# Layer 0 of a two-layer decoder trunk: transposes by VectorE's 32x32 blocks and a DRAM scratch in place of TensorE

## The chip, the cores and the metric

The kernel runs on one core of one Trainium2 chip, in one launch. The metric is the device time of that core in microseconds: the median of the runs, beside one profiled execution, whose times the trace holds. The engines named below are TensorE (PE; its weight loads are shown apart as PEld), VectorE (DVE), ScalarE (ACT), GpSimd (POOL) and SyncE (SP), which issues nearly all DMAs.

## The reference, cut to what matters

Two decoder layers over 256 tokens of width 2048, in float32. Each layer is a token mixer and a gated MLP with a width-3 causal convolution on its gate branch (width 5632), each behind an RMS norm and with a residual. Layer 0's mixer, the one that is changed, is causal attention with 16 heads of 128 (the block-sparse form of the reference falls together with it, since 256 tokens are one block):

```python
q = rope(rms_norm((h @ wq).reshape(B, S, H, dh), gq), pos, rot)   # rot = 32
k = rope(rms_norm((h @ wk).reshape(B, S, H, dh), gk), pos, rot)
v = (h @ wv).reshape(B, S, H, dh)
...
p = jax.nn.softmax(s, axis=-1)       # s = q k^T * dh**-0.5, causal
o = p @ v                            # and then o @ wo
```

Layer 1's mixer is latent attention (low-rank queries, keys and values with a shared rotary key). It has transposes of its own and is not changed.

## The kernel before, in words

TensorE multiplies float32 here in three products: a weight is split into a high part (ScalarE's copy to fp32r, L125) and a rest (VectorE's subtraction, L126), activations likewise, and hi x hi, hi x lo and lo x hi are summed. The weights come as 370 units of up to 1 MB, each of four pieces of 128x512. `Stream` (L70) loads units through SP into three buffers (L90) and splits pieces into five pairs of buffers.

The order is written out by hand. A quantum is what TensorE does with one piece: in layer 0's projections `tok_major` (L254), two token tiles by three products, six matmuls; in the output projection and the MLP `feat_major` (L278), twelve matmuls of 256 columns. The loop at the end of `trunk` (L1199) goes through the quanta: it first splits pieces up to four ahead, then issues the quantum's matmuls, then whatever has been planned for this quantum: `at(q, f)` puts f behind quantum q, `first_in(q, rank, f)` puts it there too, but ahead of the others. Every engine takes its instructions in this order. So a planned step that is not ready holds up what is planned behind it on its own engine, the splits of later pieces included.

Layer 0 goes in four groups of four heads; each has 16 quanta for queries, 16 for keys, 16 for values. Behind the last quantum q of queries or keys stands `plan_heads` (L677): `evac` takes the sums out of PSUM into a tile x of 128 tokens x 2 tiles x 4 heads x 128 (q), squares (q+1, q+2) and `rstd` (q+3, GpSimd's power) make the head norms, `scaled` and `rotate` follow at q+6 to q+9. At q+11 `turned` (L480) has TensorE transpose the eight 128x128 blocks of x into PSUM, and `queries_out` or `keys_out` (L643, L652) copy from there: a high part and a rest, and one plain copy for the first 128 tokens. For the first group everything stands some quanta later.

For each head `Head.plan` (L593) places at q the scores (TensorE) and `biased` (mask and row minimum, VectorE), at q+1 the exponentials (ScalarE), at q+2 `normal` (VectorE), at q+6 `turn` (three TensorE transposes of the probabilities, L566) with `turned` (L569: copies and the rest), and at q_values `values` (products with the values) and `parted` (the output split in two parts for the next projection). In the first three groups two heads share a place, the second pair six quanta after the first, and the values stand 12 quanta after the scores. In the last group the heads come two quanta apart and run into the output projection, the values at least 8 quanta after the scores. The output projection takes heads 0 to 7 of its first eight tiles before heads 8 to 11 and then 12 to 15.

PSUM holds four accumulators, two banks for scores and values (`sc`) and two for transposes (`tp`).

Of the kernel before, what the change touches and what calls it, by code (L numbers as in the profile page):

```python
# [10 lines left out]
F32 = mybir.dt.float32  # L11
# [3 lines left out]
ALU = mybir.AluOpType  # L15
PSUM = bass.MemoryType.PSUM

P = 128
S = 256
D = 2048  # L20
NT = S // P
# [115 lines left out]
def trunk(ctx: ExitStack, tc: tile.TileContext, a, out):  # L137
    nc = tc.nc
# [5 lines left out]
    ps_acc = ctx.enter_context(tc.tile_pool(name="ps_acc", bufs=4, space=PSUM))  # L144
    ps_tp = ctx.enter_context(tc.tile_pool(name="ps_tp", bufs=2, space=PSUM))
    ps_sc = ctx.enter_context(tc.tile_pool(name="ps_sc", bufs=2, space=PSUM))
    ctx.enter_context(tc.manual_schedule())

    mm = nc.tensor.matmul
# [90 lines left out]
    def at(q, f, *args):  # L240
        side.setdefault(q, []).append((f, args))
# [4 lines left out]
    def first_in(q, rank, f, *args):  # L246
        leading.setdefault(q, [[], []])[rank].append((f, args))
# [133 lines left out]
        nc.sync.dma_start(out[:, j, :], xT[:, j, :])  # L381


    class Heads:


# [65 lines left out]
        def rotate(self, t, stages=range(4)):  # L452
            if not self.rot:
                return
            n, rot = self.n, self.rot
            hf = rot // 2
            tb, C, Sn = self.tabs
            ct = tb[:, C + t * rot : C + (t + 1) * rot]
            st = tb[:, Sn + t * rot : Sn + (t + 1) * rot]
            x = self.x[:, t]  # L460
            def over(s):
                return s[:, None, :].to_broadcast([P, n, s.shape[1]])

            def part(name):
                r = att_pool.tile([P, 16 * 32], F32, name=name, bufs=2)
                return r[:, : n * rot].rearrange("p (n r) -> p n r", n=n)

            if 0 in stages:
                self.rot_parts = part("ro1"), part("ro2")
            t1, t2 = self.rot_parts  # L470
            if 0 in stages:
                nc.vector.tensor_tensor(t1, x[:, :, :rot], over(ct), op=ALU.mult)
            if 1 in stages:
                nc.vector.tensor_tensor(t2[:, :, :hf], x[:, :, hf:rot], over(st[:, :hf]), op=ALU.mult)
            if 2 in stages:
                nc.vector.tensor_tensor(t2[:, :, hf:], x[:, :, :hf], over(st[:, hf:]), op=ALU.mult)
            if 3 in stages:
                nc.vector.tensor_tensor(x[:, :, :rot], t1, t2, op=ALU.add)

        def turned(self, dst, pair, i0):  # L480

            tp = ps_tp.tile([P, 512], F32, name="tp")
            flat = self.x.rearrange("p t n d -> p t (n d)")
            for i in range(2):
                for t in range(NT):
                    c = (i0 + i) * P
                    nc.tensor.transpose(  # L487
                        tp[:, (i * NT + t) * P : (i * NT + t + 1) * P], flat[:, t, c : c + P], ident
                    )
            pair["tp"] = tp  # L490
# [8 lines left out]
    class Head:  # L499
# [32 lines left out]
                mm(second, qr[:, P:], kr[:, part], start=False, stop=part == 1, **flags)  # L532

        def biased(self):
            self.s = att_pool.tile([P, 3 * P], F32, name="s", bufs=3)
            self.st = small.tile([P, 6], F32, name="sst")
            masked = mask
            if self.apart:
                masked = self.s
                nc.vector.tensor_tensor(self.s[:, :P], self.sc[:, 3 * P :], mask[:, :P], op=ALU.add)  # L540
            for c, n, k, m in ((P, S, 1, mask), (0, P, 0, masked)):
                nc.vector.tensor_tensor_reduce(
                    out=self.s[:, c : c + n], in0=self.sc[:, c : c + n], in1=m[:, c : c + n],
                    scale=1.0, scalar=3e38, op0=ALU.add, op1=ALU.min,
                    accum_out=self.st[:, k : k + 1],
                )
# [16 lines left out]
        def turn(self):  # L563
# [2 lines left out]
                nc.tensor.transpose(tp[:, c * P : (c + 1) * P], self.s[:, c * P : (c + 1) * P], ident)  # L566
            self.tp = tp

        def turned(self):  # L569

            self.pT = att_pool.tile([P, 2, S], F32R, name="pT", bufs=2)
            self.pT1 = att_pool.tile([P, P], F32, name="pT1", bufs=2)
            hi, lo = self.pT[:, 0], self.pT[:, 1]
            nc.scalar.copy(hi, self.tp[:, :S])
            nc.scalar.copy(self.pT1, self.tp[:, S : 3 * P])
            nc.vector.tensor_tensor(lo, self.tp[:, :S], hi.bitcast(F32), op=ALU.subtract)

        def values(self):
            o = ps_sc.tile([P, 512], F32, name="sc")
# [13 lines left out]
        def plan(self, q, q_values, q_turn=None):  # L593


            q_turn = q_turn or q + 6
            at(q, self.scores)
            at(q, self.biased)

            late = self.rope is not None  # L600
            at(q + 1 + (late and q_turn == q + 6), self.exps)
            at(q + 2 + late + (late and q_turn == q + 6), self.normal)
            first_in(q_turn, 1, self.turn)
            first_in(q_turn, 1, self.turned)
            first_in(q_values, 0, self.values)
            first_in(q_values, 0, self.parted)
# [5 lines left out]
    env = {}  # L612
# [39 lines left out]
    def keys_out(dst, tp, i0, gain=None):  # L652
# [5 lines left out]
        copied(k0[i0 // 2], src[:, :, :P], gain)  # L658
        rest_of(lo, src, hi, gain)

    def evac_parts(state, key, scale):
        v0, v1 = env[key]
        hi, lo = v0[:, 0], v0[:, 1]
        first_, second = (state["acc"][t][:, :512] for t in range(NT))
        if scale is None:
            nc.scalar.copy(hi, first_)
            nc.vector.tensor_tensor(lo, first_, hi.bitcast(F32), op=ALU.subtract)
            nc.scalar.copy(v1, second)
            return
        r = scale()  # L670
        nc.scalar.activation(hi, first_, AF.Copy, scale=r[:, 0:1])
        nc.vector.scalar_tensor_tensor(
            lo, first_, r[:, 0:1], hi.bitcast(F32), op0=ALU.mult, op1=ALU.subtract
        )
        nc.scalar.activation(v1, second, AF.Copy, scale=r[:, 1:2])

    def plan_heads(q, hs, key, out):  # L677

        at(q, hs.evac)
        for t in range(NT):  # L680
            at(q + 1 + t, hs.squares, t)
        at(q + 3, hs.rstd)
        for t in range(NT):
            at(q + 6 + 2 * t, hs.scaled, t)
            at(q + 7 + 2 * t, hs.rotate, t)
        for i0 in (0, 2):
            pair = {}
            q1 = q + 11
            at(q1, lambda hs=hs, p=pair, i0=i0: hs.turned(None, p, i0))
            at(q1, lambda p=pair, i0=i0, key=key: out(env[key], p["tp"], i0))  # L690

    at(-1, n1.scaled, 0)
    def signed_gains():
# [11 lines left out]
    for g in range(4):  # L705
        for kind in "qkv":
            state = {"first": g == 0 and kind == "q"}
            for kt in range(KD):
                q = add(tok_major, state, lambda: n1.h, kt, KD - 1)
                if g == 0 and kind == "q" and kt + 1 < KD:  # L710
                    first(q + 1, n1.scaled, kt + 1)
                if g == 0 and kind == "k" and kt < 12:
                    for j in range(kt * 4 // 3, (kt + 1) * 4 // 3):
                        at(q, n1.square, j)
                        at(q + 1, n1.total, j)
            if g == 0 and kind == "q":
                at(q + 14, n1.sums)
            if kind == "q":
                at(q, moba_tiles, g)
            if kind == "v":  # L720
                at(q, evac_parts, state, ("v", g), lambda: n1.rstd)
                q_v = q
            else:
                hs = Heads(state, 4, P, G_Q if kind == "q" else G_K, 32, (tab, T_MC, T_MS), lambda: n1.rstd)
                plan_heads(q + (0 if g else 15 if kind == "q" else 9), hs, ("qT" if kind == "q" else "kT", g),
                           queries_out if kind == "q" else keys_out)
                q_k = q
        for i in range(4):
            hd = Head(
                4 * g + i, lambda g=g: env["qT", g], lambda g=g: env["kT", g], lambda g=g: env["v", g],  # L730
                i, lambda: env["oT"], parts=True,
            )
            if g < 3:

                q0 = q_k + (14 if g else 22) + i // 2 * 6
                hd.plan(q0, q0 + 12)
            else:
                q0 = q_k + 14 + 2 * i
                hd.plan(q0, max(q0 + 8, q_v + 3 + i))


    def plan_wo(norm, order):
# [301 lines left out]
    class Rotary:  # L1044
# [6 lines left out]
        def out(self, i):  # L1051
            heads = env["qrT"][:, 4 * (self.i0 // 2) + 2 * i : 4 * (self.i0 // 2) + 2 * i + 2]
            tp = self.pair["tp"].rearrange("p (a s) -> p a s", a=2)
            rows, rest = (slice(k * 64, (k + 1) * 64) for k in (i, 1 - i))
            nc.scalar.copy(heads[rows], tp[rows])
            nc.vector.tensor_tensor(heads[rest], tp[rows], heads[rows].bitcast(F32), op=ALU.subtract)
# [263 lines left out]
```

## Time and profile before

| What | Value |
|---|---|
| median of three runs | 2083.99 us (2083.98 to 2084.32) |
| profiled execution, its span | 2081.8 us |
| TensorE busy | 2076.9 us, 16742 matmuls |
| VectorE busy | 1415.0 us (68%) |
| ScalarE busy | 1148.0 us (55%) |
| DMA | 391.82 MB, of it 2.10 MB written to HBM |
| granted TensorE clock | 1.000 |

The span runs from the first to the last instruction. Layer 0's projections and heads lie at about 0 to 320 us, its output projection up to 391 us. Busy time is the time in which an engine has an instruction under way; matmuls are pipelined, so a mean length of one says more than its slot. In the groups of instructions a row has line, engine, operation, out<-in, the shapes and the count, then busy us and mean ns, then the engine's idle time just before with what ended it. In the chain and the timeline a row has the start in us, the length in us, and what. A row of DMA issues has the count, the size of one and the median time from issue to landing.

### The profile page before, as it was taken

To read this page: it belongs to the slowest core of one execution; us is meant where nothing else is said; L and a number is where in the kernel's file an instruction comes from. 1 tells how busy PE (TensorE), PEld (TensorE's weight loads), DVE (VectorE), ACT (ScalarE), POOL (GpSimd) and SP (SyncE) were. 2 spreads that over 40 slices of the span, in tenths; PEclk is the share of its full clock that TensorE was granted. 3 is DMA by queue.
4 is the path that set the end of the run, shared out by engine and by line. 5 is a ranking of instruction groups with operands and counts; after the bars stand their busy time and mean duration, and the time that the engine had idled before them with its cause. 6 is when DMAs were issued, how large, how long until landed. Compare 5 with 4: busy or idle time off the path is not lost.

```text
span 2081.8 us, 42114 instructions
## 1 busy us (share of the span) xinstructions
PE 2076.9 (100%) x16742; PEld 2011.4 (97%) x16742; DVE 1415.0 (68%) x2915; ACT 1148.0 (55%) x2248; POOL 46.1 (2%) x36
## 2 busy tenths in 40 slices
PE   9999999999999999999999999999999999999999
PEld 7888889999999999999999889999999999999999
DVE  6877676776666766655556898766667666755554
ACT  6555555555555555555455786655555555544443
POOL 0000000000000000000000110000000000000000
PEclk9999999999999999999999999999999999999999
DMA  7445445555555555555554533555555555555553
GB/s 271 174 173 180 166 162 203 183 193 192 200 187 201 186 199 193 193 202 184 201 194 159 203 124 123 195 190 196 190 202 186 200 189 196 196 198 207 198 205 132
DMA packets 59269, 391.82 MB, mean 188 GB/s; under 512 B 6832, under 2 KB 9520, under 8 KB 13248
## 3 DMA queue, kind: packets, MB, share of 16 engines
q1 hardware_dynamic: 58896, 388.83, 51.7%
q8 instruction: 131, 2.15, 0.4%
q14 instruction: 66, 0.54, 0.1%
q10 hardware_dynamic: 144, 0.26, 0.0%
q0 software_dynamic: 32, 0.04, 0.0%
HBM read 387.01 MB, written 2.10 MB: 187 GB/s over the span
## 4 chain that ended last, share of the span: by engine, by line
PE 100%; DMA 0%; issue 0%; ACT 0%; DVE 0%; POOLq 0%
PE acc L288 26%; PE acc L290 26%; PE acc L289 26%; PE acc L262 18%; PE tp L487 1%; PE tp L566 1%; PE sc L495 0%; PE sc L496 0%; PE sc L494 0%; PE sc L584 0%; PE sc L516 0%; DMA par<-in_par 0%; PE sc L532 0%; PE sc L530 0%; PE tp L357 0%; PE sc L527 0%
## 5 line engine op out<-in xcount | busy, mean ns | idle before, releaser
L126 DVE TENSOR_TENSOR wlo<-raw,whi 128x512 fp32r<-128x512 f32 (+1 forms) x1464 | 996.9, 689 | 375.5 <-ACT whi L125 373.6
L125 ACT CAST whi<-raw 128x512 fp32r<-128x512 f32 (+1 forms) x1463 | 871.2, 620 | 466.9 <-PE acc L289 213.1
L288 PE MATMUL acc<-h,whi 128*128 128x256 f32 x2880 | 795.4, 276 | 0.0
L290 PE MATMUL acc<-h,wlo 128*128 128x256 f32 x2880 | 795.0, 276 | 0.0
L289 PE MATMUL acc<-h,whi 128*128 128x256 f32 x2880 | 794.9, 276 | 0.0
L289 PEld LDWEIGHTS acc<-h,whi 128*128 128x128 f32 x2880 | 540.7, 188 | 0.0
L288 PEld LDWEIGHTS acc<-h,whi 128*128 128x128 f32 x2880 | 540.6, 188 | 0.0
L290 PEld LDWEIGHTS acc<-h,wlo 128*128 128x128 f32 x2880 | 540.6, 188 | 0.0
L288 PE MATMUL acc<-a,whi 128*128 128x256 f32 x1408 | 388.6, 276 | 0.0
L290 PE MATMUL acc<-a,wlo 128*128 128x256 f32 x1408 | 388.6, 276 | 0.0
L289 PE MATMUL acc<-a,whi 128*128 128x256 f32 x1408 | 388.6, 276 | 0.0
L262 PE MATMUL acc<-whi,h 128*128 128x512 f32 (+1 forms) x896 | 268.1, 378 | 0.4 <-ACT h L310 0.4
L289 PEld LDWEIGHTS acc<-a,whi 128*128 128x128 f32 x1408 | 264.3, 188 | 0.0
L290 PEld LDWEIGHTS acc<-a,wlo 128*128 128x128 f32 x1408 | 264.3, 188 | 0.0
L288 PEld LDWEIGHTS acc<-a,whi 128*128 128x128 f32 x1408 | 264.3, 188 | 0.0
L262 PEld LDWEIGHTS acc<-whi,h 128*128 128x128 f32 x896 | 164.8, 188 | 30.3 <-ACT h L310 0.9
L262 PE MATMUL acc<-wlo,h 128*128 128x512 f32 (+1 forms) x448 | 168.4, 376 | 0.0
L288 PE MATMUL acc<-oT,whi 128*128 128x256 f32 x512 | 142.7, 279 | 0.0
L290 PE MATMUL acc<-oT,wlo 128*128 128x256 f32 x512 | 141.6, 277 | 0.0
L289 PE MATMUL acc<-oT,whi 128*128 128x256 f32 x512 | 141.5, 276 | 0.0
L808 DVE TENSOR_TENSOR g<-acc,rstd_b 128x256 f32<-128x256 f32 x88 | 37.5, 426 | 126.0 <-PE acc L290 123.1
L815 ACT ACTIVATE c<-g,par 128x256 f32<-128x256 f32 x88 | 53.1, 603 | 108.0 <-DVE g L808 108.0
(190 smaller groups left out, 1633.7 us busy)
## 6 DMA issues: line engine op xcount, KB each, us to landing
raw<-in_ffn_gu SPq DMA_DIRECT2D x176, 1024.0 KB, 4.8
raw<-in_ffn_down SPq DMA_DIRECT2D x88, 1024.0 KB, 4.8
raw<-in_moba_wk SPq DMA_DIRECT2D x16, 1024.0 KB, 4.8
raw<-in_moba_wv SPq DMA_DIRECT2D x16, 1024.0 KB, 4.8
raw<-in_moba_wo SPq DMA_DIRECT2D x16, 1024.0 KB, 4.8
raw<-in_mla_wo SPq DMA_DIRECT2D x16, 1024.0 KB, 4.8
raw<-in_moba_wq SPq DMA_DIRECT2D x12, 1024.0 KB, 4.8
raw<-in_mla_wkv_a SPq DMA_DIRECT2D x8, 576.0 KB, 3.6
```

What stands on the lines that cost most here:

```text
L125: self.nc.scalar.copy(hi[:, :n], w)
L126: self.nc.vector.tensor_tensor(lo[:, :n], w, hi[:, :n].bitcast(F32), op=ALU.subtract)
L262: mm(state["acc"][t][:, :n], src[:, kt, c : c + P], (t_lo if part == 1 else t_hi)[:, :n], start=kt == 0 and part == 0, stop=kt == k_last a ...
L288: mm(o, w_hi, src[:, kt, :S], start=first and k == 0, stop=False, skip_group_check=True)
L289: mm(o, w_hi, src[:, kt, S:], start=False, stop=False, skip_group_check=True)
L290: mm(o, w_lo, src[:, kt, :S], start=False, stop=kt == k_last, skip_group_check=True)
L487: nc.tensor.transpose(tp[:, (i * NT + t) * P : (i * NT + t + 1) * P], flat[:, t, c : c + P], ident)
L566: nc.tensor.transpose(tp[:, c * P : (c + 1) * P], self.s[:, c * P : (c + 1) * P], ident)
L808: nc.vector.tensor_tensor(self.g[:, 2:], self.gate["acc"][:, :S], self.norm.rstd_b, op=ALU.mult)
L815: nc.scalar.activation(self.c, self.g[:, 2:], AF.Identity, bias=par[:, cb : cb + 1], scale=self.cw(2))
```

## The change

In layer 0 alone the TensorE transposes go. For queries and keys, `cross` (at q+9) has VectorE transpose x in blocks of 32x32 within each 32 partitions (one instruction for each of the two token tiles) into a tile b; four DMAs, one for each 32 partitions, write it to a scratch in DRAM, and `crossed` (q+11) reads it back into x with one DMA, so that the blocks change places between the partitions. At q+16 `crossed_queries` or `crossed_keys` make high part, rest and plain copy from x in SBUF. For the probabilities the same stands at q+3 (one block transpose and four DMAs a head), q+5 (one DMA) and, two quanta ahead of the values, `turned`. All these DMAs are issued by SP. `scaled` and `rotate` stand one quantum earlier (q+5 to q+8). The heads' scores stand four quanta later than before (five in the first group), the values 12 after the scores in the last group too. Probability tiles have four buffers in place of three; the rotation's temporaries take n x rot numbers in place of 512. Layer 1 calls the old functions.

```diff
+    dram = ctx.enter_context(tc.tile_pool(name="dram", bufs=2, space=bass.MemoryType.DRAM))
...
+    def cross_out(srcs, b):
+
+        w = b.shape[1] // P
+        there = dram.tile([4, 32, 4, w * 32], F32, name=f"there{w}")
+        to = b.rearrange("p (j n t c) -> p t n j c", j=4, t=len(srcs), c=32)
+        for t, src in enumerate(srcs):
+            nc.vector.transpose(to[:, t], src.rearrange("p (n j c) -> p n j c", j=4, c=32))
+        for i in range(4):
+            nc.sync.dma_start(
+                there.rearrange("j a i m -> i a j m")[i],
+                b[32 * i : 32 * (i + 1)].rearrange("a (j m) -> a j m", j=4),
+            )
+        return there
+
+    def cross_in(dst, there):
+        nc.sync.dma_start(dst, there.rearrange("j a i m -> (j a) (i m)"))
...
-                r = att_pool.tile([P, 16 * 32], F32, name=name, bufs=2)
-                return r[:, : n * rot].rearrange("p (n r) -> p n r", n=n)
+                r = att_pool.tile([P, n * rot], F32, name=name, bufs=2)
+                return r.rearrange("p (n r) -> p n r", n=n)
...
+        def cross(self):
+
+            b = att_pool.tile([P, NT * 4 * P], F32, name="blk", bufs=1)
+            self.there = cross_out([self.x[:, t].rearrange("p n d -> p (n d)") for t in range(NT)], b)
+
+        def crossed(self):
+            cross_in(self.x.rearrange("p t n d -> p (t n d)"), self.there)
...
-            self.s = att_pool.tile([P, 3 * P], F32, name="s", bufs=3)
+            self.s = att_pool.tile([P, 3 * P], F32, name="s", bufs=4 if self.parts else 3)
...
+        def cross(self):
+            b = att_pool.tile([P, 3 * P], F32, name="sblk", bufs=2)
+            self.there = cross_out([self.s], b)
+
+        def crossed(self):
+            cross_in(self.s, self.there)
+            self.tp = self.s.rearrange("p (i n c) -> p n i c", i=4, n=3)
...
+            if self.parts:
+                at(q + 1, self.exps)
+                at(q + 2, self.normal)
+                at(q + 3, self.cross)
+                at(q + 5, self.crossed)
+                first_in(q_values - 2, 1, self.turned)
+                first_in(q_values, 0, self.values)
+                first_in(q_values, 0, self.parted)
+                return
...
+    def crossed_queries(dst, hs):
+
+        q0, q1 = dst
+        src = hs.heads_of().rearrange("p (n t) i c -> p t n i c", t=NT)
+        hi, lo = (q1[:, part].rearrange("p n (i c) -> p n i c", c=32) for part in range(2))
+        nc.scalar.copy(hi, src[:, 1])
+        nc.vector.tensor_tensor(lo, src[:, 1], hi.bitcast(F32), op=ALU.subtract)
+        nc.scalar.copy(q0.rearrange("p n (i c) -> p n i c", c=32), src[:, 0])
+
+    def crossed_keys(dst, hs):
+
+        k0, k = dst
+        for b in range(2):
+            src = hs.heads_of()[:, 4 * b : 4 * b + 4]
+            hi, lo = (k[b][:, part].rearrange("p n (t i c) -> p (n t) i c", t=NT, c=32) for part in range(2))
+            nc.scalar.copy(hi, src)
+            nc.vector.tensor_tensor(lo, src, hi.bitcast(F32), op=ALU.subtract)
+            nc.scalar.copy(k0[b].rearrange("p n (i c) -> p n i c", c=32), src[:, 0::2])
...
-            at(q + 6 + 2 * t, hs.scaled, t)
-            at(q + 7 + 2 * t, hs.rotate, t)
-        for i0 in (0, 2):
-            pair = {}
-            q1 = q + 11
-            at(q1, lambda hs=hs, p=pair, i0=i0: hs.turned(None, p, i0))
-            at(q1, lambda p=pair, i0=i0, key=key: out(env[key], p["tp"], i0))
+            at(q + 5 + 2 * t, hs.scaled, t)
+            at(q + 6 + 2 * t, hs.rotate, t)
+        at(q + 9, hs.cross)
+        at(q + 11, hs.crossed)
+        at(q + 16, lambda: out(env[key], hs))
...
-                           queries_out if kind == "q" else keys_out)
+                           crossed_queries if kind == "q" else crossed_keys)
...
-                q0 = q_k + (14 if g else 22) + i // 2 * 6
+                q0 = q_k + (18 if g else 27) + i // 2 * 6
                 hd.plan(q0, q0 + 12)
             else:
-                q0 = q_k + 14 + 2 * i
-                hd.plan(q0, max(q0 + 8, q_v + 3 + i))
+                q0 = q_k + 18 + 2 * i
+                hd.plan(q0, q0 + 12)
```

In `Head.turned` the copies read the view `self.tp` of the tile s, in place of PSUM, where `self.parts` is set.

More of the change, by code (lines that the diff above doesn't have):

```diff
@@ L478, in rotate, with heads_of @@
                 nc.vector.tensor_tensor(x[:, :, :rot], t1, t2, op=ALU.add)
+        def cross(self):
[3 more added lines that the diff above has]
+            cross_in(self.x.rearrange("p t n d -> p (t n d)"), self.there)
+        def heads_of(self):
+            x = self.x.rearrange("p t n d -> p (t n d)")
+            return x.rearrange("p (i m c) -> p m i c", i=4, c=32)
         def turned(self, dst, pair, i0):
@@ L573, in turned @@
             hi, lo = self.pT[:, 0], self.pT[:, 1]
-            nc.scalar.copy(hi, self.tp[:, :S])
-            nc.scalar.copy(self.pT1, self.tp[:, S : 3 * P])
-            nc.vector.tensor_tensor(lo, self.tp[:, :S], hi.bitcast(F32), op=ALU.subtract)
+            if self.parts:
+                hi, lo = (x.rearrange("p (n i c) -> p n i c", n=2, i=4) for x in (hi, lo))
+                first_, second = self.tp[:, :2], self.tp[:, 2]
+                pT1 = self.pT1.rearrange("p (i c) -> p i c", i=4)
+            else:
+                first_, second, pT1 = self.tp[:, :S], self.tp[:, S : 3 * P], self.pT1
+            nc.scalar.copy(hi, first_)
+            nc.scalar.copy(pT1, second)
+            nc.vector.tensor_tensor(lo, first_, hi.bitcast(F32), op=ALU.subtract)
         def values(self):
@@ L598, in plan @@
             at(q, self.biased)
+            if self.parts:
+                at(q + 1, self.exps)
[6 more added lines that the diff above has]
+                return
             late = self.rope is not None
```

## The prediction

> **What bounds the kernel now.** I read the page first: the span, the engines' busy time and the chain that ended last.
>
> ```profile
> span 2081.8 us, 42114 instructions
> ...
> PE 2076.9 (100%) x16742; PEld 2011.4 (97%) x16742; DVE 1415.0 (68%) x2915; ACT 1148.0 (55%) x2248; POOL 46.1 (2%) x36
> ...
> PE 100%; DMA 0%; issue 0%; ACT 0%; DVE 0%; POOLq 0%
> PE acc L288 26%; PE acc L290 26%; PE acc L289 26%; PE acc L262 18%; PE tp L487 1%; PE tp L566 1%; PE sc L495 0%; PE sc L496 0%; PE sc L494 0%; PE sc L584 0%; PE sc L516 0%; DMA par<-in_par 0%; PE sc L532 0%; PE sc L530 0%; PE tp L357 0%; PE sc L527 0%
> ```
>
> TensorE never rests, and the whole chain is TensorE. So an instruction taken from it is worth its slot in the chain, and nothing else is worth anything unless it makes TensorE wait. The transposes (L487, L566) are on that chain. How many of them lie in layer 0, from the view of the tile tp up to 420 us:
>
> ```profile
> L487 PE MATMUL tp<-ident,qk x64: 270/272/273, 64.6 to 287.0; 128*128 128x128 f32 x64
> ...
> L566 PE MATMUL tp<-ident,s x48: 270/273/273, 92.0 to 313.0; 128*128 128x128 f32 x48
> ```
>
> The 272 ns is the length of one pipelined instruction, not its slot. The slot is read from the chain in order of time, two pieces of it (start, length, what):
>
> ```profile
> 165.62 0.66 PE tp L566 x6
> 166.27 8.19 PE acc L262 x36
> ...
> 175.63 15.02 PE acc L262 x66
> 190.64 0.87 PE tp L487 x8
> 191.52 21.78 PE acc L262 x96
> ```
> ```profile
> 301.40 0.33 PE tp L566 x3
> ```
>
> Eight transposes take 0.87 us, the six of a pair of heads 0.66, the three of one head 0.33. Thirty-six products are six quanta in 8.19 us, so a quantum of this stage is 1.365 us; that is the unit of the plan.
>
> **What the change removes.** Eight groups of queries or keys at 0.87 us are 6.96; six pairs of heads at 0.66 are 3.96; the last four heads at 0.33 are 1.32. Sum 12.24 us, all of it on the path. The profiled execution spans 2081.8 us and the median run is 2084.0, so 2.2 us lie around the span; I carry these over. With nothing lost elsewhere the time is 2084.0 - 12.2 = 2071.8 us. This is also the best case: I see no wait of TensorE in this stage that could go too.
>
> **What it adds, and where it can hurt.** The data now go VectorE, DRAM, SBUF, and only then to the copies that TensorE waits for. The question is whether each arrives before its due quantum. Durations for this come from the groups of instructions up to 420 us:
>
> ```profile
> L637 DVE TENSOR_TENSOR k<-tp,k 128x512 fp32r<-128x512 f32 x8 | 5.5, 691 | 8.9 <-ACT k L630 8.6
> ...
> L576 DVE TENSOR_TENSOR pT<-tp,pT 128x256 fp32r<-128x256 f32 x16 | 6.8, 423 | 5.7 <-ACT pT L575 5.2
> ...
> L123 DVE CAST whi<-raw 128x512 fp32r<-128x512 f32 x1 | 0.4, 426 | 3.6 <-DMA raw<-in_moba_wq 3.6
> ...
> L630 ACT CAST k<-tp 128x512 fp32r<-128x512 f32 x8 | 4.8, 597 | 10.2 <-PE tp L487 10.2
> ```
>
> No block transpose is in this trace. The nearest rows are VectorE's pass over 128x512 (0.69 us) and its cheapest such pass (0.43); twice the former, 1.38, is my upper bound. I take 0.69, and 0.55 for 128x384, between 0.42 and 0.69. That is 16 x 0.69 + 16 x 0.55 = 20 us more for VectorE. Has it room?
>
> ```profile
> core 0: us, PE busy (x) PEld busy (x) DVE busy (x) ACT busy (x) POOL busy (x), PEclk, DMA share, GB/s
> ...
> 180.00:195.00 15.00, 15.00 (x72) 12.48 (x72) 12.75 (x40) 7.52 (x15) 1.94 (x1) 1.00 0.55 205
> 195.00:210.00 15.00, 15.00 (x68) 12.43 (x67) 11.45 (x40) 7.89 (x13) 1.95 (x1) 1.00 0.60 211
> 210.00:225.00 15.00, 15.00 (x77) 12.68 (x76) 10.13 (x30) 9.57 (x24) 0.00 (x0) 1.00 0.39 140
> ```
>
> It is busy 10.1 to 12.8 of 15 us; 1.4 more in the worst window make 14.1. Full, not over, and the split parts are four quanta (5.5 us) ahead of TensorE, which evens out a window. So this costs nothing by itself; what it does to the dates is counted below. The later copies read SBUF in place of PSUM and are as many elements; I cost that at nothing.
>
> The transfers, from the DMA issues and the queue's timeline:
>
> ```profile
> raw<-in_moba_wk SPq DMA_DIRECT2D x16, 1024.0 KB, 4.8
> ...
> out<-xT SPq DMA_DIRECT2D x16, 128.0 KB, 1.8
> ```
> ```profile
> 1.18 0.42 SPq L106 DMA_DIRECT2D raw<-in_moba_wq  x1
> 1.65 0.42 SPq L199 DMA_DIRECT2D xT<-in_xT  x1
> 2.11 0.91 SPq L106 DMA_DIRECT2D raw<-in_moba_wq  x2
> ...
> 188.37 6.14 SPq L90 DMA_DIRECT2D raw<-in_moba_wv  x2
> ```
>
> An issue every 0.46 us; a write to DRAM of 128 KB in rows of 1 KB lands in 1.8 us. The line through 128 KB (1.8) and 1024 KB (4.8) gives, as an estimate, 1.5 us for 48 KB, 2.0 for 192 KB, 3.1 for 512 KB.
>
> Queries and keys. Count from E, the end of quantum q+9 on TensorE. For the queries that were turned at 190.64 (after q+11), E is 190.64 - 2 x 1.365 = 187.91. The last rotation stood then on VectorE at
>
> ```profile
> 188.84 0.29 DVE L478 TENSOR_TENSOR qk<-ro,ro 128x128 f32<-128x128 f32 x1
> ```
>
> and ended at 189.13. It moves one quantum up, with one subtraction (L126) sliding behind it, so the block transposes begin where it ended, at E+1.2, and end at E+2.6. Four issues bring the last to E+4.0, its landing to E+5.8; a weight load issued at 188.37, just ahead, is to land at E+5.3 and does not push this much. The read back is issued at E+5.9 and lands at E+9.0. Quantum q+16, where the copies stand, ends at E+9.55: 0.55 us in hand, and for queries ScalarE and VectorE have the four quanta besides. Keys are tighter: head 0 is scored at q+18, E+12.3, and its block needs 0.60 (ScalarE) and 0.69 (VectorE) from E+9.6, so it is ready at E+10.9: 1.4 us in hand.
>
> Probabilities. Count from S, the start of a pair's scores. In before these rows belong together:
>
> ```profile
> 155.13 0.22 PE sc L516 x2
> ```
> ```profile
> 160.74 0.55 DVE L558 TENSOR_SCALAR s<-s,sst 128x128 f32<-128x128 f32 x2
> ```
>
> The second normalisation ends at 161.29, S+6.2. A subtraction (0.69) and two transposes (0.55 each) end at S+7.4 and S+8.0. Eight issues run to S+10.7 and the reads come behind them; the second head's writes land at S+12.2, its read at S+14.3, its copies and subtraction are done 1.1 later. Its values are due 12 quanta and the scores (1.15) after S, at S+17.5: 2.1 us in hand. For the second pair of a group a weight load falls between writes and reads and may push them by 4.8 - 1.8 = 3.0, while the other pair's values move its date by 1.15: 0.3 in hand. In the last group the heads come one by one and the queue takes them in series: 4 x 0.46 + 1.5 + 0.46 = 3.8 us each against 3.3 that TensorE gives, 1.5 late at the last head, still inside 2.1.
>
> The queue. SP now waits in order for VectorE and for the writes, and behind it stand the weight loads, for which everything waits. What they have in hand:
>
> ```profile
> SPq L90 <- DVE wlo L126: 305.0, 57, 7.9
> ```
> ```profile
> ACT whi L125 <- PE acc L262: 10.3, 15, 0.7
> ```
>
> A load is issued as soon as its buffer is free (SP waits for VectorE), and needed two units, 8 quanta or 10.9 us, later; it takes 4.8. So 6 us are free, and ScalarE, which splits it, waits for TensorE and not for data. The longest hold here is from the transposes to the last read's issue, 4 us for a pair and 3 for queries and keys. Cost nothing; it would start to cost over 6 us.
>
> **Sum.** -12.2 on the path, and all dates met by 0.3 to 2.1 us. Some of the 24 arrivals will miss by a little; I allow 1 us (between 0 and 4). Forecast 2084.0 - 12.2 + 1.0 = 2072.8 us; its own range is 2070.3 to 2076.
>
> **Rivals.** Let L be the lateness of the arrivals over my estimate. It costs TensorE, for keys, 4 x (L - 1.4); for second pairs, 3 x (L - 0.3); for first pairs 3 x (L - 2.1); once L - 0.6 for the last group.
>
> Small writes are slow. The probabilities go out in rows of 96 numbers, 384 B; no write like this is in the trace. If each lands in 3.0 us in place of 1.5, pairs come 1.5 late: 3 x 1.2 = 3.6, and the last group's series grows from 3.8 to 5.3 a head, 1.5 x 4 - 2.1 = 3.9 more. That gives 2071.8 + 7.5 = 2079.3 us. For it: size; against it: the bytes are few. The Trainium skill (DMA: Bandwidth & Descriptors, Specifications) speaks against the change here: it puts the least size for line rate at 512 B, and says that below it the DMA engine reads, modifies and writes. No run here has shown it yet.
>
> Everything lands late. The writes of the trace land at the end of the kernel, with no loads about; in layer 0 the engines are 39 to 60% taken. If L is 3 throughout, TensorE loses 6.4 + 8.1 + 2.7 + 2.4 = 19.6: 2091.4, slower. The point where it turns is L = 2.2 (3.2 + 5.7 + 0.3 + 1.6 = 10.8), nearly what is gained.
>
> The writes wait for one another. The four writes of a transfer interlace in the scratch. If each waits for the landing before, a pair's eight take 8 x 1.9 = 15 us in place of 5.2, L = 10, and TensorE loses some 80 us: 2150. Against it: the loads of neighbouring columns of one tile above are 0.46 apart, far below a landing.
>
> It does not do what it says. If TensorE's stream is held by something that the chain hides, the time stays at 2084. Busy 15.00 of 15.00 us in each window speaks against it.
>
> **Chances.** Forecast 0.62; small writes 0.16; all late 0.13; serial writes 0.04; no effect 0.05. A measurement can tell about 0.2%, 4.2 us, from no change. Faster by more than that: the forecast and most of the small-writes case (0.10), 0.72. Within: the rest of that case (0.06), no effect 0.05, a little of "all late" (0.02): 0.13. Slower: 0.15. The range runs from 2070.3 to 2085: it leaves out the slower cases and little else.
>
> **What would show it.** Right: no L487 or L566 transposes before 320 us, the span of TensorE's layer 0 shorter by 10 to 12 us, no TensorE idle time with a releaser on ScalarE or VectorE. Block transposes near 0.7 and 0.55 us; 1 KB writes landing near 1.8 us, reads of 512 KB near 3.1. Wrong: TensorE waits at L516 (keys late), at L494 or L584 (probabilities late), or at L262 for split weights with SP held. If the waits stand at L516 the transfers of keys are mis-sized; if at the values, the small writes are.

## The result and the profile after

The changed kernel takes 2095.84 us in the median of four runs (2095.13 to 2097.68), the one before 2083.98 beside it: a ratio of 1.0058 (95% interval 1.0044 to 1.0073). It is slower by 11.9 us; the forecast was 11.2 us faster. Against what was forecast without any lateness, 2071.8, some 24 us are lost.

The page of after: span, engines, and the chain by engine and by line.

```profile
span 2093.6 us, 42115 instructions
...
PE 2076.8 (99%) x16630; PEld 1999.5 (96%) x16630; DVE 1429.7 (68%) x2943; ACT 1147.6 (55%) x2240; POOL 46.1 (2%) x36
...
PE 87%; DMA 5%; DVE 4%; ACT 1%; issue 1%; SPq 1%; POOL 1%; ACTq 0%; DVEq 0%; POOLq 0%
PE acc L291 26%; PE acc L289 26%; PE acc L290 26%; PE acc L263 7%; DMA qk<-there 2%; DVE wlo L126 2%; DMA there<-blk 1%; DMA s<-there 1%; DVE qk L465 1%; SPq L393 1%; DVE blk L391 1%; POOL hr L452 0%; PE tp L518 0%; DMA raw<-in_moba_wk 0%; ACT whi L125 0%
```

TensorE has 112 instructions fewer, as it should. But the chain, all TensorE before, now runs for 13% of the span over others: the read back (qk<-there), the writes, VectorE. Busy time hides this: 2076.8 us here and 2076.9 before. The waits of the stage (0 to 420 us) say who stood where:

```profile
ACT k L730 <- DMA qk<-there: 19.2, 4, 5.9
...
ACT pT L619 <- DMA s<-there: 18.6, 11, 5.5
ACT q L720 <- DMA qk<-there: 17.8, 4, 4.6
...
PE sc L547 <- ACT k L732: 4.1, 3, 2.0
...
PE acc L263 <- ACT whi L125: 3.5, 4, 1.3
...
PE acc L263 <- DVE wlo L126: 2.4, 7, 0.7
```

ScalarE stands at its copies until the reads land, in total 55.6 us, up to 5.9 at once. TensorE waits for it in two places: at the scores (L547, the keys) and at the projections' products (L263), whose weights ScalarE and VectorE had not split. TensorE's three rows are 10.0 us and not 24, in part since the last product before a wait is shown as busy for 0.39 us, though the next can start 0.23 us after it. Counted from start to start of the projections' products, from 20 to 330 us, waits of over 0.1 us cost 15.1 us, shorter delays 3.4, and a stretch at a lower clock (last section) 1.6: 20.1 us (1.4 in the run below whose transfers nobody awaits).

The transfers themselves, from the DMA issues (KB each, median us to landing):

```profile
raw<-in_moba_wk SPq DMA_DIRECT2D x16, 1024.0 KB, 7.2
...
there<-blk SPq DMA_DIRECT2D x32, 128.0 KB, 2.6
qk<-there SPq DMA_DIRECT2D x8, 512.0 KB, 5.0
...
there<-sblk SPq DMA_DIRECT2D x64, 48.0 KB, 2.3
s<-there SPq DMA_DIRECT2D x16, 192.0 KB, 3.9
```

I had taken 1.8 for the write of 128 KB, 3.1 for the read of 512 KB, 1.5 and 2.0 for the probabilities' write and read. One crossing shows why: the queries of the third group, whose end of quantum q+9, counted in TensorE's products, is E = 193.31. VectorE, SP, ScalarE and TensorE, each from its own timeline:

```profile
194.55 1.30 DVE L391 STREAM_TRANSPOSE blk<-qk 128x512 f32<-128x512 f32 x2
```
```profile
195.87 1.77 SPq L393 DMA_DIRECT2D there<-blk  x4
197.77 0.39 SPq L90 DMA_DIRECT2D raw<-in_moba_wv  x1
201.12 0.34 SPq L400 DMA_DIRECT2D qk<-there  x1
```
```profile
200.31 0.62 ACT L125 CAST whi<-raw 128x512 fp32r<-128x512 f32 x1 [0.74 <-DVE wlo L126]
205.07 0.62 ACT L720 CAST q<-qk 128x512 fp32r<-128x512 f32 x1 [4.14 <-DMA qk<-there]
...
207.27 1.13 ACT L125 CAST whi<-raw 128x512 fp32r<-128x512 f32 x2
```
```profile
207.93 0.50 PE L263 MATMUL acc<-whi,h 128*128 128x512 f32 x1 [0.86 <-ACT whi L125]
208.66 0.50 PE L263 MATMUL acc<-wlo,h 128*128 128x512 f32 x1 [0.22 <-DVE wlo L126]
```

The block transposes end at E+2.5 and the last of the four issues begins near E+3.9 and ends at E+4.3, as dated. Then, between the writes and the read, a weight load of 1 MB goes into the same queue (197.77). The read is issued at 201.12, the moment the last write has landed, E+7.8 in place of E+5.9; it lands at 205.07, E+11.8 in place of E+9.0. ScalarE splits nothing between 200.93 and 207.27, 6.3 us, since after the wait it still has the queries' copies and the taking out of the next sums to do; four quanta ahead are 5.5 us; TensorE waits.

### The profile page after: what moved, and what is told of

Same layout as the page of the kernel before. It is cut to its first block, busy times and chain, and to the rows that moved or that the text cites. A ratio compares the mean times of both kernels' runs of the same rounds, so it can differ in the third digit from the quotient of the medians.

```text
span 2093.6 us, 42115 instructions
## 1 busy us (share of the span) xinstructions
PE 2076.8 (99%) x16630; PEld 1999.5 (96%) x16630; DVE 1429.7 (68%) x2943; ACT 1147.6 (55%) x2240; POOL 46.1 (2%) x36
## 4 chain that ended last, share of the span: by engine, by line
PE 87%; DMA 5%; DVE 4%; ACT 1%; issue 1%; SPq 1%; POOL 1%; ACTq 0%; DVEq 0%; POOLq 0%
PE acc L291 26%; PE acc L289 26%; PE acc L290 26%; PE acc L263 7%; DMA qk<-there 2%; DVE wlo L126 2%; DMA there<-blk 1%; DMA s<-there 1%; DVE qk L465 1%; SPq L393 1%; DVE blk L391 1%; POOL hr L452 0%; PE tp L518 0%; DMA raw<-in_moba_wk 0%; ACT whi L125 0%
## 5 line engine op out<-in xcount | busy, mean ns | idle before, releaser
L126 DVE TENSOR_TENSOR wlo<-raw,whi 128x512 fp32r<-128x512 f32 (+1 forms) x1464 | 998.0, 689 | 365.9 <-ACT whi L125 363.9
L263 PE MATMUL acc<-whi,h 128*128 128x512 f32 (+1 forms) x896 | 268.6, 380 | 3.5 <-ACT whi L125 3.5
L263 PEld LDWEIGHTS acc<-whi,h 128*128 128x128 f32 x896 | 165.8, 189 | 34.9 <-ACT whi L125 5.2
L263 PE MATMUL acc<-wlo,h 128*128 128x512 f32 (+1 forms) x448 | 171.6, 383 | 3.3 <-DVE wlo L126 2.4
```

What stands on the lines that cost most here:

```text
L126: self.nc.vector.tensor_tensor(lo[:, :n], w, hi[:, :n].bitcast(F32), op=ALU.subtract)
L263: mm(state["acc"][t][:, :n], src[:, kt, c : c + P], (t_lo if part == 1 else t_hi)[:, :n], start=kt == 0 and part == 0, stop=kt == k_last a ...
```

## The experiments

The theory is **late arrivals**: the data come back some 2 to 3 us or more after their dates (the eight reads of queries and keys land at E+11.3 to E+15.1 in place of E+9.0), ScalarE stands at the copies, and TensorE waits at the scores and for split weights. Its rivals: VectorE full with the block transposes, and SP holding the weight loads. Later runs ask what makes the arrivals late. All ratios are to the kernel before.

**No transfers.** The writes and the read are left out; the block transposes stay.

```diff
-        there = dram.tile([4, 32, 4, w * 32], F32, name=f"there{w}")
...
-        for i in range(4):
-            nc.sync.dma_start(
...
-        nc.sync.dma_start(dst, there.rearrange("j a i m -> (j a) (i m)"))
+        pass
```

> Leaves out all transfers through DRAM in layer 0 (VectorE still makes its block transposes; the later copies read the tile as it stands, so the attention of layer 0 is computed on wrongly arranged data; counts and shapes of all instructions but the DMAs stay). Theory 'late arrivals' (the data come back 2 to 3 us after their dates, ScalarE stands at the copies, the splits behind it are late, TensorE waits): the whole loss goes, 2072 to 2074 us. Rival 'VectorE full' (the 19 us of block transposes make VectorE the bound in some windows): most of the loss stays, 2088 to 2095 us. Rival 'weight loads held' (SP, waiting for VectorE and the writes, issues the weights too late): 2072 to 2074 us as well.

2072.68 us, ratio 0.9947 (0.9932 to 0.9961). This is 0.9 us over the 2071.8 of the best case, so VectorE does all its new work here almost for nothing:

```profile
L390 DVE STREAM_TRANSPOSE blk<-qk 128x512 f32<-128x512 f32 x16 | 10.4, 687 | 0.0
...
L390 DVE STREAM_TRANSPOSE sblk<-s 128x384 f32<-128x384 f32 x16 | 8.5, 559 | 0.0
```

"VectorE full" falls. The other two both gave this number, so they needed another run.

**Transfers that nobody awaits.** Every write and read stays in SP's queue on its date, but the reads land in other tiles; those of the probabilities take 256 of the 384 columns.

```diff
-            b = att_pool.tile([P, NT * 4 * P], F32, name="blk", bufs=1)
+            self.blk = b = att_pool.tile([P, NT * 4 * P], F32, name="blk", bufs=1)
...
-            cross_in(self.x.rearrange("p t n d -> p (t n d)"), self.there)
+            cross_in(self.blk, self.there)
...
-            cross_in(self.s, self.there)
+            spare = att_pool.tile([P, S], F32, name="spare", bufs=1)
+            nc.sync.dma_start(spare, self.there.rearrange("j a i m -> (j a) (i m)")[:, :S])
```

> All transposes, writes and reads of the changed kernel stand in the queues on its own dates, SP waits as before, but the reads land in spare tiles (of the probabilities 256 of 384 columns) and the copies take the data as they were, so nobody waits for an arrival (the attention of layer 0 is computed on wrongly arranged data). 'Late arrivals' as the cause of nearly all the loss: 2072.5 to 2075 us. If SP's waits (weight loads held) or the shared DMA engines cost by themselves: 2078 us or more.

2072.68 us, ratio 0.9946 (0.9930 to 0.9963), as without any transfer. SP's waits and the DMA issues of this run:

```profile
SPq L393 <- DVE blk L391: 45.5, 7, 8.0
...
SPq L400 <- DMA there<-blk: 17.8, 16, 2.0
```
```profile
there<-blk SPq DMA_DIRECT2D x32, 128.0 KB, 2.6
blk<-there SPq DMA_DIRECT2D x8, 512.0 KB, 5.0
...
spare<-there SPq DMA_DIRECT2D x16, 128.0 KB, 2.1
```

For comparison, SP's waits in after:

```profile
SPq L393 <- DVE blk L391: 48.8, 8, 8.0
...
SPq L400 <- DMA there<-blk: 17.7, 15, 2.1
```

SP waits as long as in after and the transfers of queries and keys are as slow (only the probabilities' reads, which move less, take 2.1 us and not 3.9), and none of it costs anything. The whole loss, 2095.84 - 2072.68 = 23.2 us, comes of awaiting the arrivals. This shows the theory and clears SP.

**Which arrivals.** Only queries and keys through DRAM, the heads' probabilities by TensorE; and the other way round.

```diff
-                i, lambda: env["oT"], parts=True,
+                i, lambda: env["oT"],
```

> Only queries and keys go through DRAM; probabilities are turned by TensorE as before (on the changed kernel's dates). 'Late arrivals': the eight big transfers are the later ones (3 us) and carry most of the loss; 7 us of transposes saved against 15 to 18 lost: 2091 to 2095 us. 'VectorE full': 10 of the 19 us of block transposes stay, about half the loss of 24: 2087 to 2090 us. 'Weight loads held': half of the holds stay, 2087 to 2090 us.

2099.49 us, ratio 1.0074 (1.0059 to 1.0089): slower than the whole change, and 4.5 us over the top of what was expected.

```diff
-            at(q + 5 + 2 * t, hs.scaled, t)
-            at(q + 6 + 2 * t, hs.rotate, t)
-        at(q + 9, hs.cross)
-        at(q + 11, hs.crossed)
-        at(q + 16, lambda: out(env[key], hs))
+            at(q + 6 + 2 * t, hs.scaled, t)
+            at(q + 7 + 2 * t, hs.rotate, t)
+        for i0 in (0, 2):
+            pair = {}
+            q1 = q + 11
+            at(q1, lambda hs=hs, p=pair, i0=i0: hs.turned(None, p, i0))
+            at(q1, lambda p=pair, i0=i0, key=key: out(env[key], p["tp"], i0))
...
-                           crossed_queries if kind == "q" else crossed_keys)
+                           queries_out if kind == "q" else keys_out)
```

> Only the probabilities go through DRAM; queries and keys are turned by TensorE as before. 'Late arrivals': the probabilities have 2 us in hand but for the second pairs, 5.3 us of transposes saved against 2 to 4 lost: 2080 to 2083 us. 'VectorE full': 8.5 of 19 us stay, some 10 us of the loss: 2087 to 2090 us. 'Weight loads held': half of the holds stay, 2087 to 2090 us.

2079.06 us, ratio 0.9977 (0.9968 to 0.9987). Against 2083.8 - 5.3 = 2078.5 the heads lose half a microsecond, which is less than the interval (some 2 us to either side) can tell from nothing, though their reads take as long as in after and ScalarE waits for them up to 4.3 us:

```profile
s<-there SPq DMA_DIRECT2D x16, 192.0 KB, 3.8
```

So the dates of the heads were good enough (from the other run they lose 2095.84 - (2099.5 - 5.3) = 1.6 us), and queries and keys carry the loss: 2099.5 - (2083.8 - 7.0) = 22.7 us.

**Later dates.** Everything that takes data from the scratch one or two quanta later.

```diff
-        at(q + 16, lambda: out(env[key], hs))
+        at(q + 18, lambda: out(env[key], hs))
...
-                q0 = q_k + (18 if g else 27) + i // 2 * 6
-                hd.plan(q0, q0 + 12)
+                q0 = q_k + (20 if g else 29) + i // 2 * 6
+                hd.plan(q0, q0 + 14)
...
-                q0 = q_k + 18 + 2 * i
+                q0 = q_k + 20 + 2 * i
```

> All of the change, but every arrival has two quanta (2.7 us) more: the copies of queries and keys at q+18, the scores two quanta later, the values 14 quanta after the scores in the first three groups. 'Late arrivals': most of the loss goes, 2073 to 2078 us. 'VectorE full': VectorE's work is the same in the same time, 2093 to 2097 us. 'Weight loads held': SP's waits are the same, 2093 to 2097 us.

2075.00 us, ratio 0.9957 (0.9940 to 0.9974). ScalarE's longest wait at keys goes from 5.9 to 2.2 us, and TensorE no longer waits at the scores; its longest wait that is left in the stage, but for one at the start, is at the products:

```profile
ACT k L730 <- DMA qk<-there: 5.3, 4, 2.2
```
```profile
PE acc L263 <- DVE wlo L126: 0.9, 2, 0.7
```

With one quantum (q+17, scores at q_k+19 and 28, values 13 after them in the first three groups):

> All dates one quantum (1.37 us) later, where two gave 2075.0 and none 2095.8. 'Late arrivals' with a fixed lateness over the dates of 2 to 3 us: some 1.4 us less at each of eight arrivals of queries and keys, 2083 to 2088 us, in between. If instead a late arrival makes the next one late (VectorE and ScalarE stand and start the next transposes late, TensorE's clock falls), the curve is steep and one quantum gives more than half: 2076 to 2082 us.

2081.57 us, ratio 0.9991 (0.9981 to 1.0000). The first quantum gives 14.3 us, the second 6.6: the second expectation, the steep curve. A late arrival costs more than its lateness, and what follows it does start late: without transfers the block transposes of the first three groups' keys and of the second group's queries end at E+4.2, E+2.4, E+2.4 and E+3.8; in after at E+6.0, E+4.2, E+4.2 and E+4.3.

**Queries or keys.** Two quanta for the queries' copies alone; and for keys, scores and values alone.

```diff
-        at(q + 16, lambda: out(env[key], hs))
+        at(q + (18 if out is crossed_queries else 16), lambda: out(env[key], hs))
```

> Only the copies of the queries stand two quanta later (q+18); keys, scores and values on the changed kernel's dates. If late queries hold ScalarE and so the splits of the weights (waits of TensorE at the projections' products, each followed by half the clock), some 9 us come back: 2084 to 2088 us. If the four quanta of split weights cover the queries, as the prediction said, nothing comes back: 2094 to 2097 us.

```diff
-        at(q + 18, lambda: out(env[key], hs))
+        at(q + (16 if out is crossed_queries else 18), lambda: out(env[key], hs))
```

The second diff is to the version with all dates two quanta later.

> Only keys, scores and values stand two quanta later; the queries on the changed kernel's date. TensorE's waits at the scores go (5 us in the trace), and what they drag behind them: 2086 to 2090 us. If keys and what follows were the whole loss (queries covered): 2075 to 2077 us.

Queries later: 2085.56 us, ratio 1.0008 (0.9998 to 1.0018). Keys later: 2086.58 us, ratio 1.0010 (1.0001 to 1.0020). They give back 10.3 and 9.3 us, together 19.5 of the 20.8 that both give. TensorE's waits, first with the queries later, then with the keys later:

```profile
PE sc L547 <- ACT k L732: 5.6, 4, 2.3
```
```profile
PE acc L263 <- ACT whi L125: 3.7, 4, 1.3
PE acc L263 <- DVE wlo L126: 3.0, 7, 0.6
```

Each version keeps the other one's wait: late keys stop TensorE at the scores, late queries at the products with weights that are not split.

**What makes the read slow.** The weight loads issued two quanta later, behind the read.

```diff
-            self.load(u + AHEAD_UNITS)
+            self.load(u + AHEAD_UNITS - (12 <= u < 48 and j < 2))
```

> The changed kernel on its own dates, but the loads of the weight units 15 to 50 are issued two quanta later, behind the read instead of between the four writes and the read. 'The load between' (the read of 512 KB takes 5 us and not 3.1 because a weight load of 1 MB, and the last write 3 to 4 us because it, stands ahead in the same queue): reads land 2 to 3 us earlier, near their dates; 2075 to 2082 us. Rival 'the transfer itself' (5 us is what such a read takes beside any weight stream, wherever the load stands): 2093 to 2098 us. Second rival 'the weights come late then' (two of the eight quanta in hand are given away): ScalarE waits for raw, 2085 us or more.

2087.94 us, ratio 1.0019 (1.0010 to 1.0028): 7.9 us better than the change, less than expected. The read takes 3.6 us, near the 3.1 that I had estimated:

```profile
there<-blk SPq DMA_DIRECT2D x32, 128.0 KB, 2.4
qk<-there SPq DMA_DIRECT2D x8, 512.0 KB, 3.6
```

So the load ahead of it in the queue is 1.4 of the 1.9 us by which the read is slow. The writes gain little (2.4 in place of 2.6). And the total lies in the range of the third expectation: ScalarE now waits for weights too (0.9 us in this row in after), so how much of what is left (2087.94 against 2072.68) is weights and how much reads that are still late (at the copies of queries and keys ScalarE waits 29.9 us, in after 37.0) is not separated here.

```profile
ACT whi L125 <- DMA raw<-in_moba_wk: 7.8, 3, 3.5
```

With the later dates as well:

> Both: all dates two quanta later and the loads behind the reads. 'The load between': the rest of the waits of the version with later dates goes, 2072.5 to 2074 us. 'The transfer itself': as the later dates alone, 2075 us. 'The weights come late then': above 2077 us.

2086.00 us, ratio 1.0012 (1.0002 to 1.0022), 11 us worse than the later dates alone. The third expectation holds here; ScalarE waits for weights, 38.1 us in these rows where it is 8.7 with the later dates alone:

```profile
ACT whi L125 <- DMA raw<-in_moba_wk: 17.2, 5, 4.1
...
ACT whi L125 <- DMA raw<-in_moba_wv: 11.1, 4, 4.2
ACT whi L125 <- DMA raw<-in_moba_wq: 9.8, 4, 4.5
```

**Another queue.** Writes and reads issued by GpSimd.

```diff
-            nc.sync.dma_start(
+            nc.gpsimd.dma_start(
...
-        nc.sync.dma_start(dst, there.rearrange("j a i m -> (j a) (i m)"))
+        nc.gpsimd.dma_start(dst, there.rearrange("j a i m -> (j a) (i m)"))
```

> The changed kernel on its own dates, all writes and reads of the scratch issued by GpSimd in place of SP. 'The load between' in the order of one queue: the read no longer stands behind the load that SP issued, reads land earlier, 2075 to 2085 us. 'The transfer itself' (sharing of the 16 engines, whatever the queue): 2092 us or more; GpSimd's slower issue may add to it.

2142.05 us, ratio 1.0280 (1.0265 to 1.0296). The read is faster, the writes are twice as slow:

```profile
there<-blk POOLq DMA_DIRECT2D x32, 128.0 KB, 5.0
qk<-there POOLq DMA_DIRECT2D x8, 512.0 KB, 3.8
```

The read lands at E+14.6 or later in all eight crossings, and TensorE loses more each time. The read's 3.8 us beside the 5.0 in SP's queue goes with the load between; the total says nothing on it, since the writes issued by GpSimd cost more than that. Part of it is clock: the mean granted clock is 0.92 from 60 to 345 us, so of the 46 us over the change up to some 23 (an estimate, (1 - 0.92) x 285) are a slower TensorE and not waiting.

**What the later dates still lose.** The first group's second pair ten quanta after the first, the last group's values at 13; the diff is to the version with all dates two quanta later.

```diff
-                q0 = q_k + (20 if g else 29) + i // 2 * 6
+                q0 = q_k + (20 if g else 29) + i // 2 * (6 if g else 10)
...
-                hd.plan(q0, q0 + 12)
+                hd.plan(q0, q0 + 13)
```

> The version with all dates two quanta later, with the first group's second pair of heads four quanta further away from the second group's queries, and the last group's values one quantum later. What that version still loses against the one without transfers (2.3 us) stands in its trace where VectorE has those heads' block transposes among the queries' scaling and rotation (1.7 us) and at the last head's values (0.8 us). If that is so: 2072.8 to 2073.8 us. If the rest is spread over all transfers: 2074.5 to 2075.5 us.

2076.65 us, ratio 0.9965 (0.9953 to 0.9976): a miss. TensorE's wait among the second group's queries shrinks from 0.9 to 0.4 us, and the moved pair's values wait in its place:

```profile
PE sc L525 <- ACT pT L619: 0.9, 1, 0.9
PE sc L526 <- DVE pT L621: 0.8, 1, 0.8
```

The version with all dates two quanta later stays the best of those that leave nothing out: 2075.0 us, 8.8 us under the kernel before, though its interval and that of this last run overlap. Where its last 2.3 us go stays open.

## Why the prediction was wrong, step by step

**What is removed.** Right. 12.2 us forecast, and where nothing waits for an arrival the gain is 2083.97 - 2072.68 = 11.3 us. That this is the forecast of 2072.8 is partly luck: its 1 us was allowed for arrivals that miss a little, and 0.9 us are lost where none is awaited, which no run explains.

**VectorE.** Right: 0.69 and 0.55 us were taken for the block transposes, 0.687 and 0.560 are measured, and they cost next to nothing by themselves. The date of the transposes' end, E+2.6, holds in six of the eight crossings of the run without transfers (E+2.3 to E+2.9); the first group's keys and the second group's queries miss it even there (E+4.2 and E+3.8).

**SP and the weight loads.** Right: the holds are free, as the run with transfers that nobody awaits shows, though for queries and keys they last 4.3 to 5.3 us from the transposes' end to the read's issue, and not 3. Whether just 6 us were in hand no run measures; two quanta (2.7 us) taken from them besides made ScalarE wait for weights.

**The transfers.** This is the step that failed. "1.5 us for 48 KB, 2.0 for 192 KB, 3.1 for 512 KB" was a line through two rows, one of weight loads with nothing but loads in the queue, the other of writes at the kernel's end with no loads about. In the stage they are 2.3, 3.9 and 5.0, and the 128 KB write 2.6 and not 1.8. The sum "its landing to E+5.8 ... lands at E+9.0" looked at the weight load ahead of the writes and missed the next one, which in seven of the eight crossings of after stands between the writes and the read. In the crossing shown the lateness is 2.0 us at the last write and 0.8 more at the read; in the median of the eight it is the other way about, 1.2 us from the last write's issue to the read's issue (3.15 where 1.9 was taken) and 1.9 at the read. That load is most of the read's part. It is not most of the write's: in the six crossings whose load was moved the same stretch still takes 2.4 to 3.6 us, and what makes the last write slow stays open.

**The dates.** "For queries ScalarE and VectorE have the four quanta besides" was wrong as well. The four quanta are 5.5 us from the moment ScalarE stops splitting, and it stops when it reaches the copies, here 1.9 us ahead of the date, and goes on 2.2 us after the data have come. Queries cost half of the loss, 10.3 us. The prediction had named this sign, waits at the products for split weights, but with SP's holds as the cause; it was ScalarE, standing at the copies.

**The rivals.** "Everything lands late" is what happened, and had 0.13; for L = 3 it gave 2091.4, with queries at nothing and without the drag of one late arrival on the next. In after the eight reads of queries and keys landed 2.3 to 6.1 us late and the probabilities cost little. So it is in part luck that 2091.4 is near 2095.84. "Small writes are slow" falls as the cause: the probabilities alone lose half a microsecond, and the writes with rows of 384 B land in 1.5 us at best and 2.3 in the median, not 3.0. The Trainium skill's rule on writes under 512 B (DMA: Bandwidth & Descriptors, Specifications) may hold, but no run here shows a price for it. "The writes wait for one another" falls: four writes are issued in 1.77 us. The chances stood too much on one side: the thin dates of queries and keys, 0.55 and 1.4 us, were thinner than the 2.8 us by which the estimate under them was off in the crossing shown.

## What to carry to other kernels

A step taken off the bound engine is worth its slot only if what replaces it arrives in time, so a latency must be read at the place in the queue where it will stand, with the big transfers that the plan puts between. If a date is thin, buy time in the plan first: two quanta on the same instructions turned +11.9 us into -8.8. And a wait on an engine that prepares for the bound one costs from the moment it stops preparing, not from the date.

## What the runs showed of the hardware

VectorE made 19 us of block transposes of float32 at the speed of a plain pass of the same size, 0.687 us for 128x512 beside 0.689 for the subtraction of L126, and cost the kernel at most 0.9 us. Unexpected was TensorE's clock. After a pause in the last group of after the granted clock falls; a table by stage, in the columns of the one above in the prediction:

```profile
core 0: us, PE busy (x) PEld busy (x) DVE busy (x) ACT busy (x) POOL busy (x), PEclk, DMA share, GB/s
283.00:286.00 3.00, 1.49 (x6) 0.71 (x5) 1.50 (x7) 3.00 (x7) 0.00 (x0) 1.00 0.02 8
286.00:290.00 4.00, 4.00 (x12) 3.13 (x11) 3.71 (x17) 1.51 (x4) 1.35 (x1) 0.57 0.73 262
290.00:294.00 4.00, 4.00 (x19) 3.28 (x18) 3.33 (x12) 1.84 (x3) 0.60 (x1) 1.00 0.74 264
```
```profile
225.00:240.00 15.00, 12.82 (x59) 9.95 (x59) 7.00 (x19) 8.27 (x22) 0.00 (x0) 1.00 0.62 240
```

TensorE is idle for 1.5 of 3 us and then runs 4 us at 0.57, in which it has 12 products where the next 4 us have 19: some 1.6 us lost on top of the wait. The run with only queries and keys through DRAM shows the same in the same place: 0.57 from 286 to 290 us, behind a wait of 2.1 us at the products. In after no other stretch of layer 0 has a lower clock, so the clock does not fall behind each wait, which the expectation for the later queries had supposed. The stage from 225 to 240 us holds the longest pause at the scores (2.0 us) and kept its clock, so the length of one pause does not settle it; what does stays open. The Trainium skill (TensorE: Matmul & The Clock Gate, Why this matters for your kernels) asks for no gaps over about 3 us between bursts; here less was enough, once in after.
